# Two of four weight sums of a seven-product MLP moved from VectorE to adding DMA transfers

## The chip, the cores and the metric

One core of a Trainium2 chip. The metric is the device time of one launch in microseconds (us). A core has TensorE (PE, with its weight loads as PEld), VectorE (DVE), ScalarE (ACT), GpSimd (POOL) and SyncE (SP), each with an instruction queue that is worked off in order; SP and ACT issue the DMA transfers of this kernel.

## The reference

One layer of a hybrid encoder, 256 tokens, width 2048, all float32. Three token mixers run side by side and are added; after them comes the MLP that the change touches:

```python
x = x + _rms_norm(mix, norm_mix_post)
hdn = square(relu(_rms_norm(x, norm_mlp_pre) @ w_mlp_up))     # (256, 8192)
x = x + _rms_norm(hdn @ w_mlp_down, norm_mlp_post)
```

## The kernel before

Every matrix product is made exact enough by splitting each float32 operand in two: `hi`, the operand rounded to the type fp32r, and `lo`, what the rounding left. ScalarE writes `hi` (L138), VectorE `lo` (L139), and TensorE adds three products, hi by hi, hi by lo and lo by hi. The weights come as one stream `wst` of raw tiles of 128 x 1024 (512 KB); each is split when it is due. There are three buffers each for raw tiles, `whi` and `wlo`.

The MLP has 8192 hidden columns, worked in four blocks q of 2048. `up(q, j)` makes one unit of 128 hidden columns from two raw tiles (two half units); its `post` adds the halves of the accumulator, applies relu and the square, and leaves the result in `hid`. `forms(q, m)` takes two such units as four quarters (two token halves by two units) and makes from them the seven left operands of a Strassen-Winograd product of 2 x 2 blocks: three quarters themselves and four sums `s`, each split into `fm` tiles.

`down(q, sb)` multiplies the block's hidden tile with half `sb` (1024 columns) of its down-projection, in the seven-product scheme: seven products where eight would be needed. Its weights are the four blocks 11, 12, 21, 22 of a 2 x 2 division, held in the raw tiles `R` (tag `raw2`, four buffers). It runs over four steps d; each step loads the four tiles (`braw`), splits seven weight operands, four of which are sums that VectorE makes in place with `add` (L1015), and gives each product six matmuls of 512 columns (L1047 to L1049). Over the four steps each product accumulates in a PSUM bank of its own; after the last, `post(f)` adds it into the result tiles y11, y12, y21, y22.

Blocks 0 to 2 go through `down`; while block q is multiplied, the units of block q + 1 are made. So the stage is a row of groups, one for each q, sb and d: seven products and four half units, eleven items, 24 groups in all. Block 3 goes through `tok` (L212), an ordinary product, whose left operands are the 16 split tiles `hp` (L1118, L1119).

What runs when is set in three steps. The list `work` gives the order of the items. `drive` calls each item's `prep` (load and split of its weights) one item ahead of its matmuls, and puts an item's evacuation (`posts`) behind the next item's matmuls. A scheduler at build time then orders each engine's queue, by program order and by its own estimate of when an operand is ready; the order within an engine is fixed from there on, and an instruction whose operand is late holds all that stand behind it on its engine.

Of the kernel before, what the change touches and what calls it, by code (L numbers as in the profile page):

```python
# [17 lines left out]
T = 256  # L18
# [31 lines left out]
def hybrid_block(ctx, tc, xt, x, gains, params, consts, lora, gup, wst, out):  # L50
# [28 lines left out]

    con = cpool.tile([128, NCON], F32, name="con")  # L80
    par = cpool.tile([128, NPAR], F32, name="par")

    def C(name, r=slice(0, 128), lo=0, hi=None):
        c0, w = CC[name]
        return con[r, c0 + lo:c0 + (w if hi is None else hi)]

# [158 lines left out]
    p1 = ExitStack()  # L245
    rp = p1.enter_context(tc.tile_pool(name="rp", bufs=1))

    def g1(w=T):
# [496 lines left out]
    for br in ("sb", "fox"):  # L745
        for s in ("q", "k"):
            if br == "sb":
                continue
            lst = []
            for h in range(4):  # L750
                ps = unit1(upk)
                t = g1()
                A.activation(t, ps, AF.Copy)
                lst.append(t)
            done[br + s] = lst
        done[br + "v"] = vtok()
        if br == "sb":
            done["sb"] = True
            for i, (nme, n) in enumerate((("zx", 128), ("zy", 128), ("zz", 36))):
                ps = unit1(upk)  # L760
                z = cpool.tile([n, T], F32, name=nme)
# [156 lines left out]

    AF_ = {1: 0, 2: 1, 4: 2, 5: 3, 6: 4, 7: 5, 3: 6}
    work, ready, posts = [], [], []  # L920
    pos = [0]

    def drive():


        while pos[0] < len(work):
            while len(ready) < 2 and pos[0] + len(ready) < len(work):
                ready.append(work[pos[0] + len(ready)][0]())
            now, posts[:] = posts[:], []
            work[pos[0]][1](ready.pop(0))  # L930
            pos[0] += 1
            for f in now:
                f()
        while posts:
            posts.pop(0)()
# [56 lines left out]
    def forms(q, m):  # L992

        h = hid.pop((q, m))
        s = p2.tile([128, 4, 128], F32, tag="sfm", name=nm("sfm"), bufs=1)
        V.tensor_tensor(s[:, 0], h[:, 2], h[:, 3], ALU.subtract)
        V.tensor_tensor(s[:, 2], h[:, 0], h[:, 3], ALU.subtract)
# [9 lines left out]
    def down(q, sb):  # L1007
# [6 lines left out]
        def add(a, b):  # L1014
            V.tensor_tensor(R[a], R[a], R[b], ALU.add)  # L1015
# [24 lines left out]

        def run(f, d, hl):
            if d == 0:
                Q[f] = gps() if f in (1, 3, 5) else mps()
            for i in range(2):
# [8 lines left out]
        def acc(y, p, op=ALU.add):  # L1053
            V.tensor_tensor(y, y, p, op)

        def post(f):
            new = q == 0
            if f == 1:
                if new:
                    A.activation(y11, Q[1], AF.Copy)  # L1060
                else:
                    acc(y11, Q[1])
            elif f == 5:
                if new:
                    A.activation(y12, Q[5], AF.Copy, scale=-1.0)
                    A.activation(y22, Q[5], AF.Copy, scale=-1.0)
                else:
                    acc(y12, Q[5], ALU.subtract)
                    acc(y22, Q[5], ALU.subtract)
                acc(y12, Q[3], ALU.subtract)  # L1070
            elif f == 6:

                v = vx["v"] = junk()
                A.activation(v, Q[6], AF.Copy)
                acc(v, Q[1], ALU.subtract)
                acc(y12, v)
            elif f == 7:
                acc(vx["v"], Q[7], ALU.subtract)
                acc(y22, vx["v"])
            elif f == 2:  # L1080
                acc(y11, Q[2])
            elif f == 4:
                if new:
                    A.activation(y21, Q[4], AF.Copy)
                else:
                    acc(y21, Q[4])
                acc(y21, vx["v"], ALU.subtract)
# [6 lines left out]
    for j in range(KT):  # L1094
        work.extend(up(0, j))
        if j % 2:
            work.append((lambda: None, lambda _, m=j // 2: posts.append(lambda: forms(0, m))))
    drive()
    ys.extend(p2.tile([128, D], F32, tag="y", name=nm("y"), bufs=2) for _ in range(2))
    for q in range(3):  # L1100
        for sb in range(2):
            for d, F in enumerate(down(q, sb)):
                ua, ub = (up(q + 1, 8 * sb + 2 * d + j) for j in range(2))
# [4 lines left out]
    drive()  # L1108

    wpos[0] = base + 3 * 64 + 32  # L1110
    hp = []
    for m in range(8):
        h = hid.pop((3, m))
        for i in range(2):
# [4 lines left out]
            V.tensor_tensor(t[:, T:].rearrange("p (s t) -> p s t", s=2), src, hi.bitcast(F32), ALU.subtract)  # L1119
            hp.append(t)  # L1120
    g4, loads = gain(1, [pk() for _ in range(4)])
# [147 lines left out]
```

## Time and profile before

| | us |
|---|---|
| median of 3 runs (lowest, highest) | 1608.07 (1606.12, 1613.35) |
| profiled execution | 1608.3 |
| its span | 1606.5 |
| TensorE busy | 1562.1 |
| VectorE busy | 1194.4 |
| ScalarE busy | 926.7 |
| POOL busy | 45.3 |
| first product of the stage that changes to its last | 977.66 to 1502.50 |

Times in the profile count from the span's start. A busy share is the union of an engine's instructions, and neighbours overlap by some 0.1 us; a TensorE that is "busy" need not be at its peak rate, so its rhythm (the distance between like instructions) says more. The granted clock of TensorE was 1.00 in the stage. L numbers are lines of the kernel before; the change moves them (L138 and L139 become L140 and L141, L1015 becomes L1022).

### The profile page before, as it was taken

How to read it: one execution, taken by the hardware profiler on the slowest of the kernel's cores; microseconds unless marked ns; L12 is line 12 of the kernel's file. 1: busy time of each engine (PE TensorE's matmuls, PEld its weight loads, DVE VectorE, ACT ScalarE, POOL GpSimd, SP SyncE). 2: the span in 40 equal slices, each digit the busy share in tenths (PEclk: the TensorE clock that was granted, in tenths of full speed). 3: DMA queues.
4: the chain of work that ended last, by engine and by line, in shares of the span. 5: the costliest groups of instructions: out<-in, count | busy, mean ns of one | idle time of the engine just before them, and what ended most of it. 6: DMA issues, size and time to landing. Idle time of an engine off the chain costs nothing.

```text
span 1606.5 us, 23353 instructions
## 1 busy us (share of the span) xinstructions
PE 1562.1 (97%) x8846; PEld 1317.1 (82%) x8846; DVE 1194.4 (74%) x1591; ACT 926.7 (58%) x1408; POOL 45.3 (3%) x104
## 2 busy tenths in 40 slices
PE   7999999999999999999999999999899998999997
PEld 7999999997777887788887888887688777878785
DVE  7764558874577884555555778899999999899755
ACT  7474476545675445744444766666666665666442
POOL 0030001000001000000000000000000000000000
PEclk9999999999999999999999999999999999999998
DMA  6646444453445453365685565665466655656564
GB/s 235 209 132 194 148 154 160 148 177 105 136 150 173 156 172 114 103 196 194 204 293 171 169 186 170 209 197 180 164 209 196 202 169 181 200 193 210 168 191 138
DMA packets 94144, 283.38 MB, mean 176 GB/s; under 512 B 9296, under 2 KB 11600, under 8 KB 94032
## 3 DMA queue, kind: packets, MB, share of 16 engines
q1 hardware_dynamic: 91200, 280.66, 53.8%
q8 instruction: 69, 1.13, 0.3%
q10 hardware_dynamic: 2832, 1.24, 0.3%
q14 instruction: 43, 0.35, 0.1%
HBM read 279.77 MB, written 2.10 MB: 175 GB/s over the span
## 4 chain that ended last, share of the span: by engine, by line
PE 83%; DVE 10%; ACT 3%; issue 3%; POOL 1%; DMA 1%; DVEq 0%; SPq 0%; POOLq 0%; ACTq 0%
PE gps L212 29%; PE gps L154 10%; PE gps L197 6%; PE gps L156 6%; PE gps L175 5%; PE gps L176 5%; PE gps L180 5%; DVE wlo L139 3%; DVE raw L1015 2%; PE mps L1047 2%; PE mps L1049 2%; PE mps L1048 2%; ACT whi L138 2%; PE gps L1047 1%; PE gps L1048 1%
## 5 line engine op out<-in xcount | busy, mean ns | idle before, releaser
L139 DVE TENSOR_TENSOR wlo<-raw,whi 128x1024 fp32r<-128x1024 f32 x590 | 716.0, 1222 | 285.6 <-ACT whi L138 235.9
L138 ACT ACTIVATE whi<-raw 128x1024 fp32r<-128x1024 f32 x590 | 619.9, 1057 | 438.0 <-PE gps L212 175.6
L212 PE MATMUL gps<-whi,pk 128*128 128x512 f32 x1144 | 295.4, 396 | 0.0
L212 PEld LDWEIGHTS gps<-whi,pk 128*128 128x128 f32 x1144 | 210.7, 188 | 45.5 <-issue 2.5
L154 PE MATMUL gps<-pk,whi 128*128 128x512 f32 x960 | 244.8, 391 | 0.2 <-ACT whi L138 0.2
L154 PEld LDWEIGHTS gps<-pk,whi 128*128 128x128 f32 x960 | 178.2, 188 | 37.6 <-ACT whi L138 1.1
L212 PE MATMUL gps<-wlo,pk 128*128 128x512 f32 x572 | 160.7, 395 | 0.0
L156 PEld LDWEIGHTS gps<-pk,wlo 128*128 128x128 f32 x1024 | 139.1, 190 | 13.8 <-DVE wlo L139 4.7
L175 PE MATMUL gps<-pk,whi 128*128 128x256 f32 x584 | 148.2, 290 | 0.0
L156 PE MATMUL gps<-pk,wlo 128*128 128x256 f32 x1024 | 143.5, 283 | 1.7 <-DVE wlo L139 1.7
L176 PE MATMUL gps<-pk,whi 128*128 128x256 f32 x584 | 144.5, 283 | 0.0
L212 PEld LDWEIGHTS gps<-wlo,pk 128*128 128x128 f32 x572 | 105.3, 188 | 22.0 <-issue 0.8
L1015 DVE TENSOR_TENSOR raw<-raw,raw 128x1024 f32<-128x1024 f32 x96 | 117.0, 1219 | 0.8
L175 PEld LDWEIGHTS gps<-pk,whi 128*128 128x128 f32 x584 | 112.0, 192 | 2.3 <-issue 1.7
L176 PEld LDWEIGHTS gps<-pk,whi 128*128 128x128 f32 x584 | 112.1, 192 | 0.9 <-issue 0.2
L1047 PE MATMUL mps<-whi,fm 128*128 128x512 f32 x192 | 78.2, 407 | 10.3 <-ACT whi L138 10.0
L180 PE MATMUL gps<-pk,wlo 128*128 128x256 f32 x584 | 82.7, 283 | 0.0
L180 PEld LDWEIGHTS gps<-pk,wlo 128*128 128x128 f32 x584 | 75.6, 192 | 0.0
L1049 PE MATMUL mps<-wlo,fm 128*128 128x512 f32 x192 | 75.2, 392 | 0.0
L1048 PE MATMUL mps<-whi,fm 128*128 128x512 f32 x192 | 75.1, 391 | 0.0
L197 PE MATMUL gps<-whi,pk 128*128 128x512 f32 x264 | 72.2, 396 | 0.0
L972 ACT ACTIVATE tmp<-gps 128x256 f32<-128x256 f32 x64 | 24.4, 381 | 78.3 <-PE gps L158 78.2
(300 smaller groups left out, 1927.0 us busy)
## 6 DMA issues: line engine op xcount, KB each, us to landing
raw<-in_wst_dram SPq DMA_DIRECT2D x518, 512.0 KB, 4.1
x<-in_x_dram SPq DMA_DIRECT2D x8, 256.0 KB, 6.6
out_dram<-x SPq DMA_DIRECT2D x8, 256.0 KB, 2.7
x<-in_xt_dram SPq DMA_DIRECT2D x3, 512.0 KB, 7.4
fm<-in_gains_dram SPq DMA_DIRECT2D x4, 256.0 KB, 5.3
pk<-in_gains_dram SPq DMA_DIRECT2D x4, 256.0 KB, 4.0
con<-in_consts_dram SPq DMA_DIRECT2D x1, 640.0 KB, 8.0
x<-in_xt_dram SPq DMA_DIRECT2D x2, 256.0 KB, 3.6
```

Of the source, the lines that this page charges most:

```text
L138: A.activation(hi, raw, AF.Copy)
L139: V.tensor_tensor(lo, raw, hi.bitcast(F32), ALU.subtract)
L154: PE.matmul(ps, hi[:, i * 128:i * 128 + 128], pks[i], start=first and i == 0, stop=False)
L156: PE.matmul(ps[:, 0:T], lo[:, i * 128:i * 128 + 128], pks[i][:, 0:T], start=False, stop=False)
L175: PE.matmul(ps[:, 0:T], w, u[:, 0:T], start=h == 0 and i == 0, stop=False)
L176: PE.matmul(ps[:, 0:T], w, u[:, T:2 * T], start=False, stop=False)
L180: PE.matmul(ps[:, 0:T], lo[:, i * 128:i * 128 + 128], pks[8 * h + i][:, 0:T], start=False, stop=h == 1 and i == 7)
L197: PE.matmul(ps[tt], pks[k][:, c:c + 128], w[:, (k - k0) * 512:(k - k0) * 512 + 512], start=k == 0 and part == 0 and w is hl[0], stop=w is ...
L212: PE.matmul(ps[tt], pks[k][:, c:c + 128], w[:, (k - k0) * 512:(k - k0) * 512 + 512], start=k == 0 and part == 0 and w is hl[0], stop=False)
L1015: V.tensor_tensor(R[a], R[a], R[b], ALU.add)
L1047: PE.matmul(Q[f], a, w, start=d == 0 and i == 0, stop=False)
L1048: PE.matmul(Q[f], b, w, start=False, stop=False)
```

## The change

1. Of the four weight sums of a step, two stay on VectorE and two become DMA transfers that POOL issues and that add a tile of SBUF to another (`dma_add`). The seven products are written in another, equivalent form: 3 on block 22, then 22 += 12; 7 on it, then 22 += 11, and 12 += 11 by DMA; 1 on 11; 6 on 22, then 22 += 21 by DMA; 2 on 21; 5 on 12; 4 on 22. The order of the items in a group becomes 3, half unit, 7, 1, half unit, 6, 2, half unit, 5, half unit, 4, so that other items lie between a transfer and the product that takes its result.
2. `raw2` has six buffers instead of four. Room for them comes from the constants (all but the identity matrix) and three small tiles, which move to a pool that ends before the MLP; the constants are loaded in two transfers.
3. `forms` makes two of its four sums in one instruction, and the calls of `forms` are placed one by one inside the next groups instead of two at a group's end. The splits of the last block (`split3`) are placed in the same way, and the first two weight tiles of `tok` are split ahead of the last four of them.
4. `drive` looks one real item ahead; items that only queue an evacuation no longer count.
5. The evacuations follow the new form; their number per engine stays (in block 0, seven by VectorE, and eleven in the others).

```diff
-    con = cpool.tile([128, NCON], F32, name="con")
+    ident = cpool.tile([128, 128], F32, name="ident")
...
+    con = rp.tile([128, NCON - 128], F32, name="con")
...
-    side.append(lambda: nc.sync.dma_start(out=con, in_=consts))
+    side.append(lambda: nc.sync.dma_start(out=con, in_=consts[:, 128:]))
+    side.append(lambda: nc.sync.dma_start(out=ident, in_=consts[:, 0:128]))
...
-        raw = p2.tile([128, HALF], F32, tag="raw2", name=nm("raw"), bufs=4)
+        raw = p2.tile([128, HALF], F32, tag="raw2", name=nm("raw"), bufs=6)
...
-        V.tensor_tensor(s[:, 0], h[:, 2], h[:, 3], ALU.subtract)
-        V.tensor_tensor(s[:, 2], h[:, 0], h[:, 3], ALU.subtract)
-        V.tensor_tensor(s[:, 1], h[:, 0], s[:, 0], ALU.add)
-        V.tensor_tensor(s[:, 3], s[:, 1], h[:, 1], ALU.subtract)
+        V.tensor_tensor(s[:, 0:2], h[:, 0:4:2], h[:, 3:4].to_broadcast([128, 2, 128]), ALU.subtract)
+        V.tensor_tensor(s[:, 2], h[:, 0], s[:, 1], ALU.add)
+        V.tensor_tensor(s[:, 3], s[:, 2], h[:, 1], ALU.subtract)
...
+        def dma_add(a, b):
+            G.dma_start(out=R[a], in_=R[b], accum_op=ALU.add)
+
         def prep(f, d):
-            if f == 1:
-                R["11"], R["12"] = braw(q, c0, d, "11"), braw(q, c0, d, "12")
+            if f == 3:
+                R["22"], R["12"] = braw(q, c0, d, "22"), braw(q, c0, d, "12")
+                r = parts(R["22"])
+                add("22", "12")
+            elif f == 7:
+                R["11"] = braw(q, c0, d, "11")
+                r = parts(R["22"])
+                add("22", "11")
+                dma_add("12", "11")
+            elif f == 1:
                 r = parts(R["11"])
-                add("11", "12")
-            elif f == 3:
-                R["22"] = braw(q, c0, d, "22")
-                r = parts(R["22"])
-            elif f == 5:
-                r = parts(R["11"])
-                add("11", "22")
-                add("22", "12")
             elif f == 6:
                 R["21"] = braw(q, c0, d, "21")
-                r = parts(R["11"])
-            elif f == 7:
                 r = parts(R["22"])
-                add("11", "21")
+                dma_add("22", "21")
             elif f == 2:
                 r = parts(R["21"])
+            elif f == 5:
+                r = parts(R["12"])
             else:
-                r = parts(R["11"])
+                r = parts(R["22"])
             return r
...
-                work.extend([F[1], ua[0], F[3], F[5], ua[1], F[6], F[7], ub[0], F[2], ub[1], F[4]])
-                if sb and q < 2:
-                    for m in (2 * d, 2 * d + 1):
-                        work.append((lambda: None, lambda _, q=q, m=m: posts.append(lambda: forms(q + 1, m))))
+                fs = [old.pop(0) if old else None for _ in range(2)]
+                for it in (F[3], ua[0], fs[0], F[7], F[1], ua[1], F[6], F[2], ub[0], fs[1], F[5], ub[1], F[4]):
+                    if it:
+                        work.append(it)
+                if sb:
+                    for m in (2 * d, 2 * d + 1):
+                        old.append(later(lambda q=q, m=m: forms(q + 1, m) if q < 2 else split3(m)))
+    work.append((None, lambda _: first3()))
+    work.extend(old)
```

What this does to the queues is shown at three places. First VectorE in a group of block 1 (raw_11236 is before's tile 11, raw_11238 its 12, raw_11270 its 22). Before, with three of the four sums of the group in twelve rows:

```order
L1015 TENSOR_TENSOR raw_11236<-raw_11236,raw_11238 128x1024
L973 TENSOR_TENSOR tmp_11253<-gps_11186,tmp_11252 128x256
L139 TENSOR_TENSOR wlo_11261<-raw_11258,whi_11260 128x1024
L139 TENSOR_TENSOR wlo_11273<-raw_11270,whi_11272 128x1024
L996 TENSOR_TENSOR sfm_12018<-pk_11167 128x128
L139 TENSOR_TENSOR wlo_11294<-raw_11236,whi_11293 128x1024
L998 TENSOR_TENSOR sfm_12018<-pk_11167,sfm_12018 128x128
L1015 TENSOR_TENSOR raw_11236<-raw_11236,raw_11270 128x1024
L139 TENSOR_TENSOR wlo_11308<-raw_11305,whi_11307 128x1024
L1015 TENSOR_TENSOR raw_11270<-raw_11270,raw_11238 128x1024
L139 TENSOR_TENSOR wlo_11320<-raw_11236,whi_11319 128x1024
L999 TENSOR_TENSOR sfm_12018<-sfm_12018,pk_11167 128x128
```

And VectorE in such a group after (raw_11408 is 22, raw_11410 is 12, raw_11441 is 11, raw_11488 is 21):

```order
L141 TENSOR_TENSOR wlo_11413<-raw_11408,whi_11412 128x1024
L1022 TENSOR_TENSOR raw_11408<-raw_11408,raw_11410 128x1024
L981 TENSOR_TENSOR tmp_11424<-gps_11359,tmp_11423 128x256
L141 TENSOR_TENSOR wlo_11432<-raw_11429,whi_11431 128x1024
L141 TENSOR_TENSOR wlo_11444<-raw_11408,whi_11443 128x1024
L1022 TENSOR_TENSOR raw_11408<-raw_11408,raw_11441 128x1024
L141 TENSOR_TENSOR wlo_11467<-raw_11441,whi_11466 128x1024
L141 TENSOR_TENSOR wlo_11479<-raw_11476,whi_11478 128x1024
L141 TENSOR_TENSOR wlo_11491<-raw_11408,whi_11490 128x1024
L141 TENSOR_TENSOR wlo_11512<-raw_11488,whi_11511 128x1024
L981 TENSOR_TENSOR tmp_11522<-gps_11449,tmp_11521 128x256
L141 TENSOR_TENSOR wlo_11531<-raw_11528,whi_11530 128x1024
```

Two sums stand at the group's head, and from there on only splits and unit sums. The other two sums are now on POOL, which had nothing in this stage before:

```order
L1025 DMA raw_11222<-raw_11303 128x1024
L1025 DMA raw_11410<-raw_11441 128x1024
L1025 DMA raw_11408<-raw_11488 128x1024
L1025 DMA raw_11595<-raw_11626 128x1024
L1025 DMA raw_11593<-raw_11674 128x1024
```

The second and third row are those of the group above. Second, ScalarE, which waits for them: before, the `hi` splits of a group's second half (DVE in brackets: a wait for VectorE; DMAHW: for a load):

```order
L138 ACTIVATE whi_11319<-raw_11236 128x1024 [waits DVE_49,PE_49,Activation_49]
L138 ACTIVATE whi_11339<-raw_11270 128x1024 [waits DVE_49,PE_49,Activation_49]
L972 ACTIVATE tmp_11350<-gps_11276 128x256 [waits PE_49]
L138 ACTIVATE whi_11359<-raw_11357 128x1024 [waits DMAHW6_49,Activation_49]
L138 ACTIVATE whi_11369<-raw_11317 128x1024 [waits DMAHW7_49,DVE_49,PE_49]
L974 ACTIVATE tmp_11351<-tmp_11351 128x256 [waits DVE_49]
L138 ACTIVATE whi_11392<-raw_11390 128x1024 [waits DMAHW0_49,PE_49,Activation_49]
L978 ACTIVATE pk_11355<-tmp_11351 128x2x128 [waits Activation_49]
L138 ACTIVATE whi_11402<-raw_11236 128x1024 [waits DVE_49,PE_49]
```

After, the same place (DMASW: a wait for an adding transfer):

```order
L140 ACTIVATE whi_11490<-raw_11408 128x1024 [waits DVE_49,PE_49,Activation_49]
L140 ACTIVATE whi_11511<-raw_11488 128x1024 [waits DMAHW6_49,DVE_49,PE_49]
L980 ACTIVATE tmp_11521<-gps_11449 128x256 [waits PE_49]
L140 ACTIVATE whi_11530<-raw_11528 128x1024 [waits DMAHW1_49,DVE_49]
L982 ACTIVATE tmp_11522<-tmp_11522 128x256 [waits DVE_49]
L140 ACTIVATE whi_11540<-raw_11410 128x1024 [waits DMASW4_49,DMAHW2_49,PE_49,Activation_49]
L986 ACTIVATE pk_11526<-tmp_11522 128x2x128 [waits Activation_49]
L140 ACTIVATE whi_11563<-raw_11561 128x1024 [waits DMAHW3_49,PE_49]
L140 ACTIVATE whi_11573<-raw_11408 128x1024 [waits DMASW5_49,DVE_49,PE_49]
```

The splits for products 5 (raw_11410) and 4 (raw_11408) now wait for transfers, with an evacuation and a half unit's split between and behind them. Third, VectorE at the end of the stage, before (L1119 are the last block's splits, the L139 rows the first weights of `tok`):

```order
L1054 TENSOR_TENSOR y_9448<-y_9448,mps_13613 128x512
L1119 TENSOR_TENSOR fm_14212<-pk_13535,fm_14212 128x256
L1054 TENSOR_TENSOR y_9448<-y_9448,junk_14111 128x512
L1119 TENSOR_TENSOR fm_14215<-pk_13723,fm_14215 128x256
L1119 TENSOR_TENSOR fm_14218<-pk_13723,fm_14218 128x256
L1119 TENSOR_TENSOR fm_14221<-pk_13908,fm_14221 128x256
L1119 TENSOR_TENSOR fm_14224<-pk_13908,fm_14224 128x256
L1119 TENSOR_TENSOR fm_14227<-pk_14097,fm_14227 128x256
L1119 TENSOR_TENSOR fm_14230<-pk_14097,fm_14230 128x256
L139 TENSOR_TENSOR wlo_14242<-raw_14239,whi_14241 128x1024
L139 TENSOR_TENSOR wlo_14249<-raw_14246,whi_14248 128x1024
L139 TENSOR_TENSOR wlo_14268<-raw_14265,whi_14267 128x1024
```

And after (L1117 and L141):

```order
L1065 TENSOR_TENSOR y_9442<-y_9442,mps_13555 128x512
L981 TENSOR_TENSOR tmp_14192<-gps_14127,tmp_14191 128x256
L141 TENSOR_TENSOR wlo_14200<-raw_14197,whi_14199 128x1024
L141 TENSOR_TENSOR wlo_14206<-raw_14203,whi_14205 128x1024
L1065 TENSOR_TENSOR y_9442<-y_9442,mps_13591 128x512
L1117 TENSOR_TENSOR fm_14211<-pk_13904,fm_14211 128x256
L1065 TENSOR_TENSOR y_9442<-y_9442,junk_14117 128x512
L1117 TENSOR_TENSOR fm_14214<-pk_13904,fm_14214 128x256
L1117 TENSOR_TENSOR fm_14217<-pk_14103,fm_14217 128x256
L1117 TENSOR_TENSOR fm_14220<-pk_14103,fm_14220 128x256
L141 TENSOR_TENSOR wlo_14244<-raw_14241,whi_14243 128x1024
L141 TENSOR_TENSOR wlo_14263<-raw_14260,whi_14262 128x1024
```

Four of the sixteen small splits are left there, and the first two weight splits of `tok` stand ahead of them.

More of the change, by code (lines that the diff above doesn't have):

```diff
@@ L84, in C @@
         c0, w = CC[name]
-        return con[r, c0 + lo:c0 + (w if hi is None else hi)]
+        if name == "ident":
+            return ident[r, lo:w if hi is None else hi]
+        return con[r, c0 - 128 + lo:c0 - 128 + (w if hi is None else hi)]
     def P(name, i=0, r=slice(0, 128)):
@@ L760, in hybrid_block @@
                 ps = unit1(upk)
-                z = cpool.tile([n, T], F32, name=nme)
+                z = rp.tile([n, T], F32, name=nme)
                 shift(ps, MU_X + i, z, n)
@@ L906, in hybrid_block @@
             upk2.append(u)
-    AF_ = {1: 0, 2: 1, 4: 2, 5: 3, 6: 4, 7: 5, 3: 6}
-    work, ready, posts = [], [], []
-    pos = [0]
+    AF_ = {1: 0, 2: 1, 4: 2, 7: 3, 5: 4, 6: 5, 3: 6}
+    work, posts, hl = [], [], {}
     def drive():
-        while pos[0] < len(work):
-            while len(ready) < 2 and pos[0] + len(ready) < len(work):
-                ready.append(work[pos[0] + len(ready)][0]())
+        while work:
+            prep, run = work.pop(0)
+            if prep is None:
+                run(None)
+                continue
+            for w in [(prep, run)] + [w for w in work if w[0]][:AHEAD]:
+                if w not in hl:
+                    hl[w] = w[0]()
             now, posts[:] = posts[:], []
-            work[pos[0]][1](ready.pop(0))
-            pos[0] += 1
+            run(hl.pop((prep, run)))
             for f in now:
@@ L1042, in run @@
             if d == 0:
-                Q[f] = gps() if f in (1, 3, 5) else mps()
+                Q[f] = gps() if f in (3, 7, 1) else mps()
             for i in range(2):
@@ L1054, in acc, with first @@
             V.tensor_tensor(y, y, p, op)
-        def post(f):
[L1057 to L1070, printed above, removed]
+        def first(y, p, op=ALU.add):
+            if q == 0:
+                A.activation(y, p, AF.Copy, scale=1.0 if op == ALU.add else -1.0)
+            else:
+                acc(y, p, op)
+        def post(f):
+            if f == 3:
+                first(y12, Q[3], ALU.subtract)
+            elif f == 1:
+                first(y11, Q[1])
             elif f == 6:
```

40 lines of the change are left out of this document (23 added, 17 removed).

## The prediction

> **What bounds the kernel now.** I read the busy shares, then cut the span at the stage that changes, then looked for the rhythm of TensorE inside it, and last for what its waits end on. The page's head:
>
> ```profile
> span 1606.5 us, 23353 instructions
> PE 1562.1 (97%) x8846; PEld 1317.1 (82%) x8846; DVE 1194.4 (74%) x1591; ACT 926.7 (58%) x1408; POOL 45.3 (3%) x104
> ```
>
> Over the whole span TensorE looks like the only bound, but the change touches one stage, the seven-product part of the MLP, from its first product to its last. Cut into stretches (columns: time, then PE, PEld, DVE, ACT, POOL busy with instruction counts, granted clock, DMA share, GB/s):
>
> ```profile
> 977.66:1502.50 524.84, 510.37 (x2548) 421.62 (x2547) 499.50 (x572) 342.93 (x471) 0.00 (x0) 1.00 0.59 191
> 977.66:1070.23 92.57, 92.57 (x474) 78.80 (x473) 85.79 (x91) 60.95 (x83) 0.00 (x0) 1.00 0.60 193
> 1070.23:1172.95 102.72, 97.29 (x476) 77.59 (x475) 100.07 (x130) 70.00 (x98) 0.00 (x0) 1.00 0.57 184
> 1172.95:1225.37 52.42, 52.42 (x271) 44.86 (x270) 47.61 (x48) 33.19 (x43) 0.00 (x0) 1.00 0.62 203
> 1225.37:1352.59 127.22, 119.43 (x583) 94.91 (x582) 124.72 (x159) 80.92 (x111) 0.00 (x0) 1.00 0.57 181
> ```
>
> VectorE is busy 97 to 98% in the second and fourth of these stretches (100.07 of 102.72, 124.72 of 127.22), where TensorE has holes; in the first and third TensorE has none and VectorE has 7 to 9% to spare. So two bounds alternate. The rhythm of TensorE shows what that costs: one instruction of L158 closes each unit of the up-projection, two of them per group of eleven items (seven products, four half units).
>
> ```profile
> 1008.15 0.40 PE L158 MATMUL gps<-pk,whi 128*128 128x512 f32 x1
> 1028.85 0.40 PE L158 MATMUL gps<-pk,whi 128*128 128x512 f32 x1
> 1080.49 0.40 PE L158 MATMUL gps<-pk,whi 128*128 128x512 f32 x1
> 1102.55 0.40 PE L158 MATMUL gps<-pk,whi 128*128 128x512 f32 x1
> 1135.95 0.39 PE L158 MATMUL gps<-pk,whi 128*128 128x512 f32 x1
> 1162.80 0.40 PE L158 MATMUL gps<-pk,whi 128*128 128x512 f32 x1
> ```
>
> An undisturbed group takes 1028.85 - 1008.15 = 20.70 us, one in the second stretch 22.06, and the one across the block's end 26.85. The stage has 24 groups (3 blocks x 2 x 4): 24 x 20.70 = 496.8 us against 524.84, so 28.0 us of TensorE time are lost. The waits of the stage name the other end (engine line <- releaser: us, times, longest):
>
> ```profile
> ACT whi L138 <- DVE raw L1015: 58.4, 38, 4.7
> PEld mps L1047 <- ACT whi L138: 20.7, 29, 2.1
> ```
>
> ScalarE's split waits for VectorE's weight sum (L1015), and TensorE for that split.
>
> **VectorE's work, part by part.** The busy column overlaps neighbours, so I take the step from one start to the next:
>
> ```profile
> 1136.78 1.22 DVE L139 TENSOR_TENSOR wlo<-raw,whi 128x1024 fp32r<-128x1024 f32 x1
> 1137.91 0.42 DVE L973 TENSOR_TENSOR tmp<-gps,tmp 128x256 f32<-128x256 f32 x1
> 1138.25 1.21 DVE L139 TENSOR_TENSOR wlo<-raw,whi 128x1024 fp32r<-128x1024 f32 x1
> 1146.86 0.68 DVE L1054 TENSOR_TENSOR y<-y,junk 128x512 f32<-128x512 f32 x1
> 1147.46 0.68 DVE L1054 TENSOR_TENSOR y<-y,mps 128x512 f32<-128x512 f32 x1
> 1154.91 0.55 DVE L1003 TENSOR_TENSOR fm<-pk,fm 128x384 fp32r<-128x384 f32 x1
> 1155.38 0.28 DVE L996 TENSOR_TENSOR sfm<-pk 128x128 f32<-128x128 f32 x1
> 1155.58 0.28 DVE L997 TENSOR_TENSOR sfm<-pk 128x128 f32<-128x128 f32 x1
> ```
>
> That is 1.13 us for 1024 columns, 0.60 for 512, 0.47 for 384, 0.34 for 256, 0.20 for 128. A group before has 11 splits and 4 sums (15 x 1.13 = 16.95) and two unit sums (0.68): 17.63. A set of hidden-tile forms is 4 x 0.20 + 0.47 + 0.60 = 1.87, and two fall on each group of a block's second half: 21.37. Eleven accumulations (6.6 us) close each half, 1.65 per group: 23.0 against 20.70, a surplus of 2.3 x 4 = 9.3 per such half. In the first half it is 19.28, under 20.70, and nothing is lost there. Two halves carry forms (blocks 0 and 1), so 18.6 of the 28.0 us are explained by load alone; the rest I put down to the chain split, sum, split and to bunched forms.
>
> Edits:
> - **Two sums leave VectorE.** 48 of 96 L1015 instructions go, 2 x 1.13 = 2.26 per group.
> - **Forms.** One 256-column instruction replaces two of 128: 0.34 for 0.40, so 1.81 each. They are also handed out inside the next groups instead of two at a group's end.
> - The heavy group becomes 13 x 1.13 + 0.68 + 2 x 1.81 + 1.65 = 20.64, just level with TensorE's 20.70; the others 17.0. Bounds for what is still lost: 0 (level load), and 14 (half of the 28, if chains rather than load cause it). The first half of block 0 ran at 19.28 of 20.70 without a loss, so the level case is nearer to it than to 23.0; I take 2 us for each of the two heavy halves. **Stage: 28.0 - 4 = 24 us gained.**
> - **The adding transfers.** POOL issues two per group; POOL is idle in this stage (0.00 busy above), so only their delay counts. No row shows one. Nearest rows:
>
> ```profile
> raw<-in_wst_dram SPq DMA_DIRECT2D x518, 512.0 KB, 4.1
> L344 POOL TENSOR_TENSOR sbt<-sbt,con 128x128 f32<-128x128 f32 x8 | 8.9, 1148 | 0.8 <-DVE sbt L341 0.8
> L364 POOL TENSOR_TENSOR sbm<-sbm,con 128x128 f32<-128x128 f32 x8 | 5.5, 718 | 0.5 <-ACT sbm L361 0.5
> ```
>
> A plain 512 KB load lands 4.1 us after its issue. An add reads two tiles and writes one: 4.1 if it is as quick as a load, 12.3 if the three pass one after the other. I take two streams, 8.2. What may it take? TensorE's pieces:
>
> ```profile
> 905.03 2.00 PE L154 MATMUL gps<-pk,whi 128*128 128x512 f32 x8
> 907.82 1.78 PE L154 MATMUL gps<-pk,whi 128*128 128x512 f32 x7
> 981.81 0.40 PE L1047 MATMUL gps<-whi,fm 128*128 128x512 f32 x1
> 984.55 1.75 PE L154 MATMUL gps<-pk,whi 128*128 128x512 f32 x7
> ```
>
> A half unit is 2.79 us, a product (984.55 - 981.81) / 2 = 1.37. The sum into R12 is started beside product 7 and needed by product 5: a half, 7, 1, a half, 6, 2 and a half lie between, 4 x 1.37 + 3 x 2.79 - 1.06 for ScalarE's split = 12.8. The sum into R22 must wait for product 6's second split and is needed by product 4: 6, 2, a half, 5, a half, 3 x 1.37 + 2 x 2.79 - 1.06 = 8.6, more if VectorE runs ahead. At 8.2 both are hidden and cost 0; each us beyond 8.6 costs 24 us, because ScalarE's split for product 5 or 4 then stands in the queue with the next half's split and the unit's evacuation behind it, and TensorE behind those. SP is moved too: the load of the next R21 waits for this group's add to end, and with it the raw half unit issued after it; that half is needed about 16 us after the add's start, so at 8.2 + 4.1 it is in time.
> - **DMA engines.** In the undisturbed stretch the share is 0.62: 12.8 us of 20.70 for eight loads, 1.6 each. Two adds at one to three times that are 3.2 to 9.6; at two streams 6.4, together 19.2 of 20.70. Tight, not over. The Trainium skill, "Collectives: The Full Stack", section on the bandwidth ceiling, says that an adding transfer runs at half the rate of a copy because it reads two sources through one ring, not because of the add; by it the estimate would also be 3.2 per add and 19.2 per group, and no row here shows it.
> - **Six raw tiles for four.** Before, the first tile of a group takes the slot that product 4 of the last group frees; after, the next two loads run ahead. It pays only where the load was late; no wait of the stage on a DMA is in its list, so 0 (bounds 0 to 2).
> - **Constants** in two loads, z tiles in another pool: one more issue on SP, hidden under the start's loads: 0 (up to 0.4).
>
> **The end of the stage.** The last block's 16 splits of 256 columns move up into the groups, behind two weight splits:
>
> ```profile
> 1502.32 1.52 PE L212 MATMUL gps<-whi,fm 128*128 128x512 f32 x6
> 1507.35 2.07 PE L212 MATMUL gps<-wlo,fm 128*128 128x512 f32 x4 [3.51 <-DVE wlo L139]
> 1509.22 3.61 PE L212 MATMUL gps<-whi,fm 128*128 128x512 f32 x8
> 1513.64 1.98 PE L212 MATMUL gps<-whi,fm 128*128 128x512 f32 x8
> 1516.36 1.98 PE L212 MATMUL gps<-whi,fm 128*128 128x512 f32 x8
> 1504.06 2.10 DVE L1119 TENSOR_TENSOR fm<-pk,fm 128x256 fp32r<-128x256 f32 x6
> 1506.07 3.49 DVE L139 TENSOR_TENSOR wlo<-raw,whi 128x1024 fp32r<-128x1024 f32 x3
> ```
>
> Twelve matmuls take 2.72 us here (1516.36 - 1513.64), 0.227 each. From 1502.32 to 1513.64 there are 6 + 4 + 8 + 4 = 22, 5.0 us of work in 11.3: 6.3 lost, behind L1119 and the weight splits after it. Bounds of the gain 0 and 6.3; in the new order the two weight splits precede the last four small ones, so I take 5.5. In blocks 0 and 1 nothing of this applies, and the groups of block 2 take the small splits (4 x 0.34 per group) on 17.0 of load.
>
> **Sum.** 24 + 5.5 = 29.5, less 0.4 for the constants: 29. The profiled execution took 1608.3 (span 1606.5 plus 1.8), as near as nothing to the median of 1608.07. 1608.3 - 29 = 1579.3; I say **1579**. The most it can be is 28.0 + 6.3: 1574.
>
> **Rivals.**
> - *The add is late (slower).* Place: the wait of ScalarE's split for product 4. At 12.3 us it is 3.7 over, x 24 = 89: 1579 + 89 = 1668. The gain is gone at 29 / 24 = 1.2 over, 9.8 us. For it: transfers beside 0.6 of share. Against: 8.6 is the least slack, since VectorE now has 3.7 us per light group to run ahead.
> - *The DMA engines become the bound.* At three streams 12.8 + 9.6 = 22.4 per group, 24 x 22.4 = 538, 13 more than now: 1608 + 13 - 5.5 = 1616.
> - *Half of the stall stays* because bunched forms and accumulations still hold the splits at block ends: 14 + 5.5 gained: 1589.
> - *VectorE gains nothing.* L344 and L364 are the same operation on POOL, 1148 and 718 ns, so POOL and its neighbours can hold each other up. If issuing an add held VectorE as long as one 1148 ns operation, the 2.26 freed would be spent again: stage as before, 1608 - 5.5 = 1603. The Trainium skill, "SBUF — State Buffer", section "Who interferes with whom", has two-input VectorE instructions contend with GpSimd's reads and GpSimd's descriptor writing starved by other VectorE modes; by that page issuing writes only, which should leave these instructions alone, and no run here shows it yet.
>
> **Chances.** The forecast (4 us or so lost, up to 1586) 0.55; half of the stall 0.19; the add late 0.13; DMA engines 0.05; VectorE gains nothing 0.05; better than 1574 0.03. A change under 0.5% (8 us) can't be told from none in this kernel. Faster: 0.55 + 0.19 + 0.03 less a little of the half case, 0.75; the same: VectorE's case and the near side of the late add, 0.09; slower 0.16. Leaving out 0.03 below and 0.16 above, the range is 1573 to 1610; the likeliest case's own is 1574 to 1586.
>
> **What would show it.** Right: groups of 20.7 us also in the halves with forms, VectorE near 440 of some 500 us in the stage, no 3.5 us hole after the last product, the wait on L1015's successor mostly gone. Wrong: ScalarE's splits waiting on the transfers from raw to raw, those landing after more than 10 us, a DMA share near 1, or VectorE's 1024-column step above 1.13.

## The result, and the profile after

The changed kernel takes 1592.65 us (median of 4 runs, 1590.86 to 1596.76) against 1609.84 (1606.12 to 1613.35; four runs of before, one more than ahead of the prediction): ratio 0.9898, 95% interval 0.9882 to 0.9914. It is 17 us faster; the forecast of 1579 was 13.6 too low. Most of this study is about those 13.6.

The head of the page of the profiled execution of after, and then the stage from its first product to its last (columns as in the prediction: time, then PE, PEld, DVE, ACT, POOL busy with counts, granted clock, DMA share, GB/s):

```profile
span 1591.1 us, 23482 instructions
PE 1557.6 (98%) x8846; PEld 1317.6 (83%) x8846; DVE 1142.5 (72%) x1519; ACT 921.8 (58%) x1408; POOL 87.3 (5%) x152
978.96:1492.74 513.78, 506.31 (x2546) 422.18 (x2545) 449.32 (x512) 337.42 (x469) 41.06 (x48) 1.00 0.84 242
```

VectorE lost 50 us of work in the stage (499.50 to 449.32), as reckoned, but the stage is only 11 us shorter (524.84 to 513.78), not 24: it is still 17.0 us longer than 24 undisturbed groups (496.8), where the forecast left 4. The first matmuls of `tok`:

```profile
1492.74 1.98 PE L214 MATMUL gps<-whi,fm 128*128 128x512 f32 x8
1494.55 1.07 PE L214 MATMUL gps<-wlo,fm 128*128 128x512 f32 x4
1495.46 1.98 PE L214 MATMUL gps<-whi,fm 128*128 128x512 f32 x8
```

They run in steps of 2.72 us from the first on (1495.46 - 1492.74): the hole at the end is gone, and from here to the span's end it is 98.4 us (1591.1 - 1492.74) where it was 104.2 (1606.5 - 1502.32), 5.8 less. Stage 10.9 (counted, as here, to the first matmul of `tok`) plus end 5.8, less 1.3 because the stage began later (978.96 for 977.66), make the 15.4 between the spans.

The waits of the stage in after (engine line <- releaser: us, times, longest), of ScalarE and of SP's own queue:

```profile
ACT whi L140 <- DMA raw<-raw: 38.8, 18, 4.7
ACT whi L140 <- DVE raw L1022: 10.6, 9, 2.3
SPq L952 <- DMA raw<-raw: 262.1, 46, 9.4
```

ScalarE's split waited 58.4 us for VectorE's sum before; that is down to 10.6, but in its place it waits 38.8 us for a transfer; all 18 of these waits are for the second add of a group, the one into tile 22 that product 4 takes. SP's load queue (L952 is `braw`) waits 262.1 us for adds to free their tiles; whether that costs anything is seen below. The transfers (the third line is of L1025, the adds alone), and the share of the chain that ended last by engine:

```profile
raw<-in_wst_dram SPq DMA_DIRECT2D x518, 512.0 KB, 4.3
raw<-raw POOLq DMA_DIRECT2D x48, 512.0 KB, 6.6
DMA to landing us min/median/max: 5.3/6.6/9.9
PE 73%; issue 9%; DMA 8%; DVE 6%; ACT 2%; POOL 1%; SPq 0%; DVEq 0%; POOLq 0%; ACTq 0%
```

An adding transfer lands 6.6 us after its issue (median). That is less than the 8.2 taken and less than the 8.6 of slack, and it is waited for all the same; but the spread is wide, and four of the 24 second adds landed only after 8.7 to 9.9 us. One wait for an add that was not late by that measure, in a group of block 0 that makes forms of block 1 (times of start, duration, in brackets the idle time before and what ended it):

```profile
1092.54 0.87 POOL L1025 DMA_DIRECT2D raw<-raw  x1 [7.86 <-DVE wlo L141]
1092.77 0.40 PE L1058 MATMUL mps<-whi,fm 128*128 128x512 f32 x1
1097.28 0.61 ACT L1009 ACTIVATE fm<-sfm 128x512 fp32r<-128x512 f32 x1
1099.78 2.01 ACT L140 ACTIVATE whi<-raw 128x1024 fp32r<-128x1024 f32 x2 [1.88 <-DMA raw<-raw]
1100.87 1.23 DVE L141 TENSOR_TENSOR wlo<-raw,whi 128x1024 fp32r<-128x1024 f32 x1 [1.63 <-ACT whi L140]
1102.43 0.40 PE L1058 MATMUL mps<-whi,fm 128*128 128x512 f32 x1
1105.40 0.42 DVE L981 TENSOR_TENSOR tmp<-gps,tmp 128x256 f32<-128x256 f32 x1
1105.96 1.39 PE L156 MATMUL gps<-pk,whi 128*128 128x512 f32 x5 [0.47 <-DVE tmp L981]
```

POOL issues the add into tile 22 just ahead of product 6 (1092.77). ScalarE comes to the split for product 4 at 1097.89 (1097.28 + 0.61), 5.4 us after the issue, and stands until the add has landed, 7.2 us after it. Product 4 itself is not late (1102.43, right behind the half unit before it). But VectorE stood idle for 1.63 us behind ScalarE, all that is queued on it comes later, and 3.5 us on TensorE waits for L981, which frees the accumulator of a unit. So a wait in ScalarE's queue can cost time though the product behind it is in time. In all 18 cases ScalarE came to the split 4.0 to 6.0 us after the issue.

Not every wait costs, though. Three groups: two in which VectorE has time to spare (busy 15.15 and 18.82 us), and then the one that follows the wait just shown, with forms (columns as before):

```profile
1167.89:1188.59 20.70, 20.70 (x109) 17.72 (x107) 15.15 (x18) 11.66 (x16) 1.74 (x2) 1.00 0.75 203
1188.59:1211.33 22.74, 21.81 (x109) 17.47 (x107) 18.82 (x18) 14.22 (x19) 1.74 (x2) 1.00 0.91 274
1102.20:1124.17 21.97, 21.39 (x109) 17.48 (x107) 20.18 (x27) 14.75 (x21) 1.74 (x2) 1.00 0.83 243
```

The first came behind a wait of 1.8 us and lost nothing; three more groups of this kind behind waits of 1.7 to 2.3 us lost at most 0.1. The second came behind the longest wait, 4.7 us, for the add that landed after 9.9, and lost 2.0. The third lost 1.3 behind a wait of 1.9. Where VectorE has time to spare it catches up before TensorE needs the result, and only the late landings cost; where the forms take that time, a short wait costs too.

### The profile page after: what moved, and what is told of

The parts are those of the page before. It is cut to its first block, busy times and chain, and to the rows that moved or that the text cites. A ratio compares the mean times of both kernels' runs of the same rounds, so it can differ in the third digit from the quotient of the medians.

```text
span 1591.1 us, 23482 instructions
## 1 busy us (share of the span) xinstructions
PE 1557.6 (98%) x8846; PEld 1317.6 (83%) x8846; DVE 1142.5 (72%) x1519; ACT 921.8 (58%) x1408; POOL 87.3 (5%) x152
## 3 DMA queue, kind: packets, MB, share of 16 engines
q8 instruction: 69, 1.13, 0.3%
## 4 chain that ended last, share of the span: by engine, by line
PE 73%; issue 9%; DMA 8%; DVE 6%; ACT 2%; POOL 1%; SPq 0%; DVEq 0%; POOLq 0%; ACTq 0%
PE gps L214 29%; PE gps L156 7%; PE gps L199 6%; PE gps L177 5%; PE gps L182 5%; PE gps L178 5%; DMA raw<-raw 4%; PE gps L158 4%; DVE wlo L141 4%; DMA raw<-in_wst_dram 3%; ACT whi L140 1%; PE mps L1060 1%; PE mps L1058 1%; PE mps L1059 1%; PE gps L1060 1%
## 5 line engine op out<-in xcount | busy, mean ns | idle before, releaser
L141 DVE TENSOR_TENSOR wlo<-raw,whi 128x1024 fp32r<-128x1024 f32 x590 | 716.2, 1223 | 314.5 <-ACT whi L140 253.4
L1025 POOL DMA_DIRECT2D raw<-raw x48 | 42.0, 875 | 557.2 <-DVE raw L1022 268.2
```

What stands on the lines that cost most here:

```text
L141: V.tensor_tensor(lo, raw, hi.bitcast(F32), ALU.subtract)
```

## The experiments

The theory after the result: **the wait** of ScalarE's split for a transfer costs the missing 13 us. Rivals: **the traffic** (the transfers slow the loads and other accesses), **VectorE's load** (there is still too much on it in the groups with forms), and the bunching of forms and accumulations.

**All four sums on VectorE again**, everything else as changed:

```diff
         def dma_add(a, b):
-            G.dma_start(out=R[a], in_=R[b], accum_op=ALU.add)
+            add(a, b)
```

> The two adding transfers go back to VectorE as in-place sums at the same places; order of items, six tiles, spread forms and the new end stay. Theory A (the transfers' relief of VectorE is what shortens the groups, though a late transfer gives part of it back): a heavy group has 15 x 1.13 + 0.68 + 3.62 + 1.65 = 22.9 us of VectorE work again, so the stage goes back to some 520 to 525 us and only the end's 6.3 us stay: 1603. Theory B (the order of items and the six tiles did it, VectorE's load didn't matter): about as the changed kernel, 1593.

Measured 1597.35 us (ratio to before 0.9928, 0.9909 to 0.9947), between the two. Two groups with forms, and the wait of the stage:

```profile
1083.10:1125.31 42.21, 41.68 (x214) 35.36 (x213) 41.58 (x51) 29.90 (x42) 0.00 (x0) 1.00 0.62 203
ACT whi L140 <- DVE raw L1022: 15.0, 11, 2.3
```

VectorE is busy 41.58 of 42.21: here the load is the bound, and the two groups take 42.21 where 41.40 is undisturbed. The order of the items, the six tiles, the forms and the end give 11 us by themselves; the two sums moved to DMA bring only about 5 more as the change has them (the intervals of the two ratios just touch).

**No sums** of the two at all (products 5 and 4 then use tiles without their sums), and **sums made by DMA but not read** (products 5 and 4 split tiles 11 and 21 instead, while the same 48 transfers run):

```diff
-            G.dma_start(out=R[a], in_=R[b], accum_op=ALU.add)
+            pass
```
```diff
-                r = parts(R["12"])
+                r = parts(R["11"])
...
-                r = parts(R["22"])
+                r = parts(R["21"])
```

> Leaves out the two sums that the transfers make (12 += 11, 22 += 21): no transfer, no wait for one, everything else as changed. Theory A (the 17 us that TensorE still loses in the stage come from a loop through the transfer: product 6's split, transfer, product 4's split, then VectorE's queue up to the next product 6's split): stage near 500 us, 1579 to 1582. Theory B (they come from VectorE's load with bunched forms and accumulations): no change, 1590 to 1593. Theory C (the transfers' traffic, a DMA share of 0.84, makes the loads late): as A here, told apart by the next kernel.

> The transfers run as in the changed kernel, with the same sources, targets and start, but products 5 and 4 split the plain tiles 11 and 21 instead of the two sums (the result of the transfers is left unused). So the traffic stays, and only the wait of ScalarE for a transfer goes. Theory A (loop through the wait): as the kernel without sums, 1579 to 1583. Theory C (traffic, or buffers held by the transfers): as changed, 1590 to 1593. Theory B: also as changed.

Measured 1580.94 (0.9829, 0.981 to 0.9849) and 1580.71 (0.9836, 0.9816 to 0.9856). The two don't differ: the transfers as such cost nothing that shows. To wait for them costs the 12 us between 1592.65 and 1580.7 (10 to 11 by the ratios to before). SP's load queue waited 271.4 us for adds in the second of them, more than the 262.1 of the changed kernel, so that wait isn't what costs. No split of ScalarE waits for a transfer there any more, and for VectorE's sums they wait:

```profile
ACT whi L140 <- DVE raw L1022: 7.8, 6, 2.1
```

**Product 6 ahead of the second half unit**, so that the second transfer starts earlier before product 4:

```diff
-   (F[3], ua[0], fs[0], F[7], F[1], ua[1], F[6], F[2], ub[0], fs[1], F[5], ub[1], F[4])
+   (F[3], ua[0], fs[0], F[7], F[1], F[6], ua[1], F[2], ub[0], fs[1], F[5], ub[1], F[4])
```

> Product 6 is moved ahead of the second half unit of the first pair (order 3, half, 7, 1, 6, half, 2, half, 5, half, 4): one half unit, 2.79 us of TensorE, moves from before the start of the second transfer to behind it; all work stays. Theory A: heavy groups fall from 21.6 towards 20.7, 1593 to 1583. Theory B and C: no change, or worse by a microsecond or two because three products stand in a row.

Measured 1585.97 (0.9865, 0.9848 to 0.9882). The wait on transfers falls from 38.8 to 6.5 us, but another one grows:

```profile
ACT whi L140 <- DMA raw<-raw: 6.5, 9, 1.2
ACT whi L140 <- DVE raw L1022: 23.8, 19, 3.2
```

Three products now stand side by side (7, 1, 6), and their splits wait for VectorE's two sums. That this wait is what the kernel still loses against 1580.7 was not tried.

**Four raw2 tiles** with the transfers, and later **four tiles with all sums on VectorE**:

```diff
-        raw = p2.tile([128, HALF], F32, tag="raw2", name=nm("raw"), bufs=6)
+        raw = p2.tile([128, HALF], F32, tag="raw2", name=nm("raw"), bufs=4)
```

> The changed kernel with four raw2 tiles instead of six. Theory A (six tiles are needed because two tiles of a group are held until a transfer ends): the next group's loads of 22 and 12 come only after this group's second transfer, some 17 us into the group, land 4 to 5 us later, and the heavy groups lose 1 to 3 us each: 1600 to 1640. Theory B (six tiles cost and bring nothing, as the prediction put it: 0 to 2): 1592 to 1595.

> The run with all four sums on VectorE (1597.35 us with six raw2 tiles), with four tiles. If six tiles only pay because a transfer holds its tiles longer and so holds back the loads: 1596 to 1599, as with six. If six tiles pay in the new order by themselves (the order loads 22 and 12 together at a group's start, and the raw tiles of the half units queue behind them on SP): 1603 to 1616, up to the 18.5 us that four tiles cost the changed kernel.

Measured 1611.15 (1.0017, 1.0000 to 1.0035) and 1598.08 (0.993, 0.9915 to 0.9945). With the transfers two tiles fewer cost 18.5 us, without them 0.7, which is nothing. The waits of both, the transfers' kernel first:

```profile
ACT whi L140 <- DMA raw<-raw: 45.0, 16, 5.8
DVE raw L1022 <- DMA raw<-in_wst_dram: 9.0, 9, 2.8
```

```profile
ACT whi L140 <- DVE raw L1022: 14.9, 12, 2.1
DVE raw L1022 <- DMA raw<-in_wst_dram: 0.9, 2, 0.5
```

An add holds two tiles for as long as it flies. With four, the loads behind them arrive late (9.0 us of VectorE's waiting, where it is 0.9 with all sums on VectorE); six tiles pay only together with the transfers. How the waits shown add up to 18.5 us isn't worked out.

**Forms bunched** at the group's end as before, and **forms of blocks 1 and 2 left out** (their products use the tiles of block 0):

```diff
-  old.append(later(...))
+  (work if q < 2 else old).append(later(...))
```
```diff
     def forms(q, m):
+        if q:
+            return
```

> The changed kernel, but the two calls of forms of a group stand at its end again, as before the change (the last block's splits stay spread). Theory A (the placing of forms matters little beside the wait): 1592 to 1596. Theory B (bunched forms were a good part of what was lost before): 1597 to 1605.

> Leaves out the forms of blocks 1 and 2 (block 0's are used again), transfers and waits as in the changed kernel: a heavy group has 3.6 us less of VectorE work, 17.0 of 20.7. Theory A' (a late transfer costs only where VectorE has no slack, since its idle time behind ScalarE's wait is then lost): the stage loses 3 to 6 us instead of 17, 1579 to 1582. Theory A'' (the transfer is too late for TensorE itself, whatever VectorE's load): 1590 to 1593.

Measured 1593.77 (0.9912, 0.9884 to 0.994): where the forms stand makes no difference that shows. And 1583.61 (0.9848, 0.9815 to 0.9882), 9 us less than the changed kernel, while ScalarE's wait on the transfers stayed as long:

```profile
ACT whi L140 <- DMA raw<-raw: 42.7, 16, 5.0
```

With less on VectorE the stage loses less. Up to 4.6 of the 9 us need no late transfer: two groups, shown in the next section, lose that by VectorE's load with forms. That the same waits also cost less fits the three groups above; how much less the profile can't say, since its execution (span 1590.1) was longer than that kernel's median and began the stage 5 us late.

**The end alone**: before, with the last block's splits placed in the groups and two weight splits ahead of them.

```diff
+            if q == 2 and sb and d:
+                ua[0], ub[0] = then(ua[0], 2 * d - 2), then(ub[0], 2 * d - 1)
...
+    drive(first3)
```

> The kernel before with the end alone changed: the last block's splits spread over its last groups, and the first two weight tiles of the ordinary product split ahead of the last of them. Theory A: the hole after the last product, 6.3 us, closes and the heavier groups of block 2 give 0 to 2 back: 1602 to 1604 where before is 1608.6. Theory B (the gain of the end depends on VectorE being relieved by the transfers): 1606 to 1609.

Measured 1604.58 (0.997, 0.9958 to 0.9983): 2.7 to 6.8 us faster, which holds the 5.8 that the end gained in after.

**Product 4 behind the next group's product 3**, first with product 6 earlier, then in the changed kernel's order:

```diff
+    old, late = [], None
...
-   (F[3], ua[0], fs[0], F[7], F[1], ua[1], F[6], F[2], ub[0], fs[1], F[5], ub[1], F[4])
+   (F[3], late, ua[0], fs[0], F[7], F[1], ua[1], F[6], F[2], ub[0], fs[1], F[5], ub[1])
...
+                late = F[4]
```

> The order of the six-earlier run (product 6 ahead of the second half unit: 1585.97 us, stage some 506 us, ScalarE's waits on transfers 6.5 us in 9 waits), and product 4 of each group also moved behind product 3 of the next one. That gives the second transfer one product and its half-waiting queue more, some 2.8 us of slack. If what that run still loses against the run whose sums are unread (501.8 us in the stage, 1580.7) is the wait for the second transfer: the waits on transfers near 0, stage 502 to 504, time 1581 to 1584. If the rest is other things (VectorE's tight load in the groups with forms, loads behind held tiles): 1585 to 1588, and more than that if the tile 22, now held longer, makes the loads wait.

> The changed kernel's order of items except that product 4 of each group stands behind product 3 of the next group; transfers, tiles and forms as in the changed kernel. Theory that the 12 us are the wait of the split for product 4 (16 of the 18 waits on transfers): the later place gives the transfer about 2.8 us more, where the longest wait was 4.7 and the mean 2.2, so most of it goes: waits on transfers below 12 us, time 1583 to 1587. Rival, that the order of the splits around product 6 is what helped in the six-earlier run and the wait only showed it: 1591 to 1594, as the changed kernel.

Measured 1586.0 (0.9854, 0.9837 to 0.987) and 1580.38 (0.9828, 0.9808 to 0.9847). Neither tests the later place: by then the next group has put its own tile into `R["22"]`, and in 18 of the 24 groups product 4 read that one, so that the transfer was seldom waited for. The second is thus one more run with unread sums, here most of the second ones. The first is no faster than the run with product 6 earlier (1585.97); in its profiled execution (1591.88 us, the longest of its four) ScalarE's splits wait for VectorE's sums instead, 69.0 us:

```profile
ACT whi L140 <- DVE raw L1022: 69.0, 34, 2.8
```

The second has 50.1 us of the same wait and still takes 1580.38, so that the sum of such waits doesn't explain the first; its cause stays open.

**The same with the right tile**:

```diff
                 dma_add("22", "21")
+                R["4"] = R["22"]
...
-                r = parts(R["22"])
+                r = parts(R["4"])
```

> The previous run of this order took 1580.38 us, but its product 4 read the next group's tile of block 22 in three groups of four, so that the second transfer's result was seldom needed. Here product 4 of each group stands behind product 3 of the next one and reads its own group's tile, into which the transfer has added. Theory that the 12 us of the changed kernel are the wait of product 4's split for a transfer that lands up to 3 us too late: a place one product later (1.4 us of TensorE, and two splits of 1.1 us on VectorE's queue ahead) takes most of that wait away: waits on transfers below 15 us, time 1582 to 1587. Rival, that the tile 22, held one product longer, delays the loads (six tiles were worth 18.5 us): the wait moves to the loads, 1588 to 1595.

Measured **1579.17 us** (1579.04 to 1581.63; ratio to before 0.9824, 0.9805 to 0.9844): 13.5 us faster than the changed kernel (12 by the ratios), and less time than was expected. Head of the page, waits and the chain's shares:

```profile
span 1577.4 us, 23491 instructions
ACT whi L140 <- DMA raw<-raw: 6.6, 3, 2.7
ACT whi L140 <- DVE raw L1022: 6.2, 6, 1.4
raw<-raw POOLq DMA_DIRECT2D x48, 512.0 KB, 7.0
PE 94%; DVE 3%; ACT 1%; POOL 1%; issue 1%; DMA 0%; SPq 0%; DVEq 0%; POOLq 0%; ACTq 0%
```

The transfers land no sooner (7.0 us), but the split comes later in ScalarE's queue: 6.6 us of waiting for 38.8, and DMA's share of the chain goes from 8% to 0, TensorE's from 73 to 94%. The six halves of the stage (four groups each, cut at the up-projection's last matmul of every fourth group), after first, then this kernel:

```profile
978.73:1060.34 81.61, 81.61 (x420) 69.66 (x419) 67.66 (x71) 53.97 (x73) 6.41 (x8) 1.00 0.83 238
1060.34:1146.12 85.78, 84.70 (x427) 70.24 (x426) 77.57 (x94) 59.51 (x85) 6.98 (x8) 1.00 0.83 242
1146.12:1232.02 85.90, 84.58 (x427) 70.39 (x426) 74.08 (x84) 54.59 (x74) 6.98 (x8) 1.00 0.84 242
1232.02:1318.90 86.88, 85.14 (x426) 70.20 (x425) 78.61 (x97) 57.93 (x81) 6.98 (x8) 1.00 0.83 246
1318.90:1406.05 87.15, 84.70 (x427) 70.23 (x425) 75.72 (x84) 54.55 (x73) 6.98 (x8) 1.00 0.84 240
1406.05:1491.12 85.07, 84.19 (x426) 70.32 (x425) 74.06 (x84) 55.69 (x81) 6.98 (x8) 1.00 0.84 244
```

```profile
977.12:1058.78 81.66, 81.66 (x420) 69.66 (x419) 67.51 (x71) 53.99 (x73) 6.41 (x8) 1.00 0.81 240
1058.78:1141.55 82.77, 82.77 (x426) 70.85 (x425) 77.36 (x93) 59.90 (x85) 6.96 (x8) 1.00 0.85 251
1141.55:1225.85 84.30, 83.78 (x427) 70.55 (x425) 74.97 (x85) 55.22 (x74) 6.96 (x8) 1.00 0.85 249
1225.85:1308.75 82.90, 82.90 (x426) 70.83 (x425) 79.14 (x97) 57.92 (x81) 6.96 (x8) 1.00 0.84 244
1308.75:1394.65 85.90, 84.29 (x427) 70.38 (x426) 75.94 (x84) 54.88 (x74) 6.96 (x8) 1.00 0.85 248
1394.65:1477.49 82.84, 82.84 (x427) 70.80 (x426) 74.75 (x84) 56.21 (x81) 6.96 (x8) 1.00 0.87 253
```

Undisturbed, a half is 4 x 20.70 = 82.8. The halves with forms (second and fourth) run at 82.77 and 82.90 here and took 85.78 and 86.88 in after: 7.0 of the 12.0 us between the stages. The third and fifth give 2.9, the last 2.2. So the waits cost most where VectorE has most to do, and something elsewhere too. By moving product 4 behind another product this run puts off both the place in ScalarE's queue and the moment at which TensorE needs the result (by one product, 1.4 us); it shows that the wait cost the 12 us, but not by itself which of the two counts.

## Why the prediction was right in direction and 13.6 us too low

- *VectorE's work* was the bound, as said. Its step has stayed at 1.13 us, its busy time in the stage is 449 (said: near 440), and the wait on its sums is mostly gone. Without the late waits the stage takes 501.75 us (977.35 to 1479.10 in the last kernel): 5.0 us lost, where 4 were forecast. That the totals agree is luck, for the place was wrong: I gave 2 us to each half with forms and they lose nothing; 4.6 of the 5 lie in the third and fifth halves (1.5 and 3.1 over 82.8), and there in one group each, the first:

```profile
1141.55:1163.77 22.22, 21.70 (x108) 17.40 (x107) 22.22 (x31) 15.67 (x22) 2.00 (x3) 1.00 0.86 252
1308.75:1332.51 23.76, 22.15 (x109) 17.23 (x108) 23.76 (x33) 15.34 (x22) 1.97 (x3) 1.00 0.87 266
```

  VectorE is busy there all the time. Since the forms are handed out one group later, the last two sets fall into this group, together with accumulations of the half before. The fourth and sixth halves begin with accumulations too, but without forms, and their first groups take 20.8 and 20.7. The sum spread the accumulations evenly over four groups (1.65 each) and so did not see this group; it also counted eleven of them for block 0, where VectorE has seven.
- *The adding transfers* are the step that failed: "At 8.2 both are hidden and cost 0". The term measured 12 us (1592.65 against 1580.71 unread). The median landing wasn't the mistake (6.6 against 8.2). Two other things were. The slack of 8.6 was counted to TensorE's need of product 4, less one split on ScalarE; but the scheduler had put the split earlier in ScalarE's queue, where it came up 4.0 to 6.0 us after the issue, and while it waits VectorE stands behind it. In the groups with forms VectorE is level with TensorE and can't make that up, so that four of them lost 0.5 to 1.3 us each behind landings of 6.1 to 7.5 us, well inside 8.6. And one landing time was taken for all 48: four second adds took 8.7 to 9.9, and the four groups behind them lost 7.3 of the 12 us. The prediction named the queue as the harm of a late add, and set the point from which it bites by TensorE alone. "8.6, more if VectorE runs ahead" came about only where VectorE has time to spare: there the add was issued up to 1.5 us ahead of product 6, in the groups with forms 0.2 to 0.6.
- *The end*: 5.8 against 5.5. *Constants*: stage begin 978.96 in after, 977.35 in the last kernel, 977.66 before; 0.4 can't be told in that spread.
- *Six raw tiles for four*, "0 (bounds 0 to 2)": worth 18.5 us in this kernel. The reason given (loads weren't late before) holds for before and for the kernel with sums on VectorE (0.7 us); the transfers changed it, since each holds two tiles. The sum wasn't hurt, because the kernel has the six.
- *The rivals.* "The add is late": right wait, right place, but in the groups with forms it bites from a landing of about 6 us and softly, not from 8.6 at 24 us for each us. Cut by halves as above, the 5.6 and 8.0 us waited in the halves with forms (38.8 in all) cost 3.0 and 4.0. "Half of the stall stays" came nearest in time (1589), but not by its cause: bunching the forms changes nothing (1593.77), and with forms and accumulations where the changed kernel has them the last kernel loses 5.0 us, not 14. "VectorE gains nothing" is refuted: the mean of its split is 1223 ns in after, 1222 before, so issuing on POOL did not hold it:

```profile
L141 DVE TENSOR_TENSOR wlo<-raw,whi 128x1024 fp32r<-128x1024 f32 x590 | 716.2, 1223 | 314.5 <-ACT whi L140 253.4
L1025 POOL DMA_DIRECT2D raw<-raw x48 | 42.0, 875 | 557.2 <-DVE raw L1022 268.2
```

- *The DMA engines* weren't the bound: 0.84 of their time, and 0.84 too over the stage of 501.75 us in the last kernel. By queue (packets, MB, share of 16 engines from 977 to 1495):

```profile
q1 hardware_dynamic: 38896, 98.64, 56.2%
q0 software_dynamic: 6912, 25.17, 26.4%
```

The 48 adds took 0.264 x 518 / 48 = 2.85 us of all engines each, the 188 weight loads of the stage at most 0.562 x 518 / 188 = 1.55. So the 3.2 per add that I took was a little high, and the ratio is at least 1.84. The Trainium skill, "Collectives: The Full Stack", section on the bandwidth ceiling, gives 2 for the adding step of a collective against its copy; the trace agrees as far as it goes.

The last kernel, whose order differs from the forecast one in product 4 alone, shows the sum without the failed term. Its span is 29.1 us under before's (1606.5 - 1577.4): the stage 22.9 (524.66 - 501.75), the end 5.9, the start 0.3, for a forecast of 24, 5.5 and -0.4, together 29.

## What to carry to other kernels

When work moves from an engine to a transfer, count the slack to the place where the consumer stands in its own queue as well as to the moment at which the bounding engine needs the result, and count it for the latest landing and not for the median. The stretch between the two is free only while the engines behind the wait have time to catch up: here waits of 1.7 to 2.3 us cost nothing in groups without forms, and one of 1.9 us was followed by a loss of 1.3 in a group with them. Where there is no such time, put the consumer later. A wait of 38.8 us in 18 pieces on an engine that is 58% busy cost 12 us here, and moving one item took it away. A transfer also holds its tiles while it flies: give it buffers for that time, and expect no gain from them where there is no transfer.

## What the runs showed of the hardware

A transfer of 512 KB that adds one SBUF tile to another landed in 6.6 us (median of 48, 5.3 to 9.9) with the DMA engines 0.84 busy; the medians of the nine kernels that have them run from 6.3 to 8.8, and the two longest belong to kernels of 1580 us. It cost POOL 0.87 us of issue. Beside the adds a plain load of 512 KB landed in 5.7 us (median of the stage), where it took 4.6 before. Neither this nor the share of 0.84 (0.59 before) touched the undisturbed rhythm of 20.7 us.
